# Hybrid retention and attention layer: the mixers' five engines in one written order

## The chip, the cores and the metric

The kernel runs on 1 core of one Trainium2 chip. The metric is the device time of one execution in microseconds (us). The kernel before takes 1167.28 us, the median of 3 runs (1166.82 to 1169.25).

## What is computed

One post-norm encoder layer in f32, with S = 1024 rows, D = 1024 and a hidden width of 2816:

```
u   = x @ W_in                                # one projection: rq rk rv rg aq ak av
ret = swish(rg) * GroupNorm(retention_fwd(rq, rk, rv) + retention_bwd(rq, rk, rv))   # 8 heads of 64
att = windowed attention(aq, ak, av)          # 8 query heads, 2 key/value heads, +-128, ALiBi, sink
h   = LN1(alpha * x + concat(ret, att) @ W_out)
f   = (silu(h @ W_gate) * (h @ W_up)) @ W_down + sigmoid(h @ W_pg) * (p @ W_pe)
out = LN2(alpha * h + f)
```

Retention is computed in chunks: within a chunk by masked scores, between chunks by a state of 64 x 64 that decays (by a scan over the chunks, once forward and once backward).

## The kernel before

**Number format.** A large matmul in f32 is made of three matmuls in a rounded format: each operand is split into a high part (a copy on ACT, which rounds) and a low part (a subtraction on DVE). `mm3` (L82 to L84) is such a triple; three matmuls with 512 columns are here called one projection *step*.

**Stages.** First comes a stretch of projection that is not touched (up to about 50 us). Then come the mixers (to about 350 us): four pairs of heads, each with retention and attention. They are laid between projection steps: `queue` holds all steps of the projections that are left, and `run` goes over a list in which F (None) stands for a *share* of steps, and everything else is a piece of a mixer (the keys' transposes K, the chunk products kv C, the scans S, scores, values, and so on). Pair 0's attention has 16 + 64 steps, pair 0's retention ("retention 0") 48, pairs 1 to 3 have 48 each, and 16 come last. Behind the mixers lie W_out, LN1, the gate, the FFN and LN2.

**Ticks.** `ticks` counts the steps that have been emitted. `take` emits a step and then all pieces in the lists `later` and `side` whose tick has come. `side` carries the splitting of later weights: of W_out (`presplit_out`), of W_pg (`presplit_gate`) and of two small ones (`presplit_small`). Each is loaded, summed where a sum is needed (DVE, L715 for W_pg), split by `put` (high part on ACT L653, low part on DVE L654) and stored to HBM by SP (L655, to `wod` or `pgd`).

**What sets the order.** In the mixers, `manual_schedule` names PE alone (L791): PE runs in the order of the source. What DVE, ACT, POOL and SP do is placed by a scheduler, with an edge (`behind`) from the newest projection step to pieces that shall not come before it. Each engine's queue, in whatever order it ends up, is then run in that order: an instruction that waits holds those behind it. SP issues the DMAs.

**What the steps below name.** L116 loads two tiles of a projection weight (tag "raw", 2 buffers), L76 and L77 split them. L418 and L424 are the keys' transposes and their decayed copies, two half tiles each (K(0), K(1)); L439 is kv, L446 and L448 its evacuation on DVE and ACT, L456 the scan and L467 the DMA that moves states. L577, L579 and L582 are an attention block's scores, their masked reduction and their exponential; L617 and L622 transposes of these and the copies ("ptr"); L634 the values. The norm of retention goes row (L530) to HBM and back: spread (L535), power (POOL, L538), store, fetch (L545), scaled (L549), at the ticks of LAGS = (3, 6, 9, 12, 15) behind it.

## Time and profile before

| | before |
|---|---|
| median of 3 runs | 1167.28 us |
| profiled execution, its time | 1168.96 us |
| its span | 1167.2 us |
| PE busy | 1151.9 us (99%) |
| DVE, ACT, POOL busy | 895.7 (77%), 564.4 (48%), 105.1 (9%) us |
| fp32 triples, first of three lines (L82) | 240 instructions, 97.2 us |

The prediction quotes the views. A row of windows gives the start and end, the length, then busy us and number of instructions for PE, PEld, DVE, ACT and POOL, then the granted clock, the busy share of the DMA engines and GB/s. A row of waits gives the engine and line that waited, what released it, and us in total, times, longest. A row of the timeline gives start, length, engine, line and operation, with the idle time ahead of it in brackets. A row of groups gives count, busy us, mean ns, and idle before. The lines are those of the kernel before.

### The profile page before, as it was taken

Reading aid. Unit: us, or ns where it says so; the run is one execution under the profiler, and the core shown is the slowest. Engines: PE = TensorE matmul, PEld = TensorE weight load, DVE = VectorE, ACT = ScalarE, POOL = GpSimd, SP = SyncE. Lnnn points to the kernel's source line nnn. Section 1 sums busy time; section 2 is a strip of 40 time slices with the busy share of each in tenths; the row PEclk is TensorE's granted clock in tenths of the full one; section 3 lists DMA queues with packets and bytes.
Section 4 is the critical chain, followed back from the end, with each engine's and each line's share of the span. In section 5 each row is a group of like instructions: output and inputs, shape, how many; then the busy total and the mean of one; then the engine's idle time right before and its main releaser. Section 6 shows DMA issues by size and latency. Waiting matters only on the chain.

```text
span 1167.2 us, 19086 instructions
## 1 busy us (share of the span) xinstructions
PE 1151.9 (99%) x6978; PEld 965.8 (83%) x6978; DVE 895.7 (77%) x1687; ACT 564.4 (48%) x1162; POOL 105.1 (9%) x118
## 2 busy tenths in 40 slices
PE   9999999999999999999999999999999999999997
PEld 7888878777888888888888888888888888888886
DVE  5556678594858898948999988888888876774778
ACT  5645367666546366214444433443344445552462
POOL 2000010102010021000000000000000011124242
PEclk9999999999999999999999999999999999999999
DMA  6346777666567955756322332332223289999978
GB/s 251 103 159 214 258 241 232 211 210 194 154 216 241 365 178 185 269 193 210 112 96 98 115 107 98 103 134 101 100 73 136 83 249 344 348 236 217 256 172 233
DMA packets 88863, 218.64 MB, mean 187 GB/s; under 512 B 12544, under 2 KB 20928, under 8 KB 88768
## 3 DMA queue, kind: packets, MB, share of 16 engines
q1 hardware_dynamic: 79984, 200.11, 49.6%
q0 software_dynamic: 8784, 17.31, 8.4%
q8 instruction: 55, 0.90, 0.3%
q14 instruction: 40, 0.33, 0.1%
HBM read 143.35 MB, written 62.19 MB: 176 GB/s over the span
## 4 chain that ended last, share of the span: by engine, by line
PE 89%; issue 4%; DMA 3%; DVE 2%; ACT 1%; SPq 1%; POOL 0%; DVEq 0%; POOLq 0%; ACTq 0%
PE bmm L875 8%; PE bmm L874 8%; PE bmm L876 8%; PE bt L874 6%; PE bt L875 6%; PE bt L876 6%; PE bmm L82 4%; PE bmm L84 4%; PE bmm L83 4%; PE bs L876 4%; PE bs L875 4%; PE bs L874 4%; PE bo L876 4%; PE bo L875 4%; PE bo L874 4%
## 5 line engine op out<-in xcount | busy, mean ns | idle before, releaser
L82 PE MATMUL bmm<-H,w 128*128 128x512 f32 x240 | 97.2, 405 | 0.1
L84 PE MATMUL bmm<-H,w 128*128 128x512 f32 x240 | 94.0, 392 | 0.5 <-issue 0.5
L83 PE MATMUL bmm<-H,w 128*128 128x512 f32 x240 | 94.0, 392 | 0.0
L1474 ACT ACTIVATE ev<-ev 128x512 f32<-128x512 f32 x42 | 26.5, 630 | 105.0 <-DVE ev L1503 91.8
L1648 POOL DMA_DIRECT2D h0b<-in_w_dn x24 | 21.6, 900 | 537.7 <-DVE ev L1454 503.6
L82 PEld LDWEIGHTS bmm<-H,w 128*128 128x128 f32 x240 | 45.2, 188 | 12.2 <-issue 1.9
L84 PEld LDWEIGHTS bmm<-H,w 128*128 128x128 f32 x240 | 45.0, 188 | 10.2
L83 PEld LDWEIGHTS bmm<-H,w 128*128 128x128 f32 x240 | 45.1, 188 | 7.8
L582 ACT ACTIVATE sc<-sc,st 128x384 f32<-128x384 f32 (+1 forms) x64 | 37.3, 586 | 17.1 <-DVE st L579 17.0
L579 DVE CUSTOM_DVE_ANT_0 sc<-cst,bs,nskb 128x384 f32<-128x384 f32 (+1 forms) x64 | 35.2, 575 | 7.0 <-PE bs L578 6.9
L1503 DVE TENSOR_TENSOR ev<-ev,bt 128x512 f32<-128x512 f32 x44 | 30.0, 682 | 12.5 <-PE bt L876 12.5
L622 ACT ACTIVATE ptr<-bt 128x384 f32<-128x384 f32 (+1 forms) x64 | 26.5, 456 | 25.5 <-PE bt L617 25.4
L1454 DVE TENSOR_TENSOR ev<-ev,bs 128x256 f32<-128x256 f32 x63 | 25.5, 416 | 15.6 <-PE bs L876 14.7
L1476 DVE TENSOR_TENSOR ev<-ev 128x512 f32<-128x512 f32 x42 | 29.0, 691 | 10.5 <-ACT ev L1474 9.0
L77 DVE TENSOR_TENSOR w<-raw,w 128x512 fp32r<-128x512 f32 x34 | 23.0, 687 | 17.3 <-ACT w L76 16.7
L874 PE MATMUL bmm<-H,u 128*128 128x512 f32 x92 | 36.1, 392 | 0.0
L875 PE MATMUL bmm<-H,u 128*128 128x512 f32 x92 | 36.0, 392 | 0.0
L876 PE MATMUL bmm<-H,u 128*128 128x512 f32 x92 | 35.8, 389 | 0.0
L874 PE MATMUL bmm<-H,w 128*128 128x512 f32 x84 | 32.9, 392 | 0.0
L875 PE MATMUL bmm<-H,w 128*128 128x512 f32 x84 | 32.9, 392 | 0.0
L876 PE MATMUL bmm<-H,w 128*128 128x512 f32 x84 | 32.7, 389 | 0.0
L1454 DVE TENSOR_TENSOR ev<-ev,bo 128x256 f32<-128x256 f32 x70 | 28.3, 416 | 5.2 <-PE bo L876 4.5
(832 smaller groups left out, 3836.8 us busy)
## 6 DMA issues: line engine op xcount, KB each, us to landing
ad<-ev SPq DMA_DIRECT2D x33, 512.0 KB, 2.6
pgd<-pro SPq DMA_DIRECT2D x28, 512.0 KB, 3.3
raw<-in_w_gu SPq DMA_DIRECT2D x22, 512.0 KB, 4.0
ln<-in_w_gu SPq DMA_DIRECT2D x22, 512.0 KB, 4.6
raw<-ad SPq DMA_DIRECT2D x40, 256.0 KB, 6.2
ln<-ad SPq DMA_DIRECT2D x37, 256.0 KB, 6.3
H<-in_w_dn SPq DMA_DIRECT2D x33, 256.0 KB, 9.2
wod<-aq SPq DMA_DIRECT2D x16, 512.0 KB, 2.7
```

The costliest lines, as they stand in the source:

```text
L82: pe.matmul(o, lh, rh, start=start, stop=False)
L83: pe.matmul(o, lh, rl, start=False, stop=False)
L84: recent[0] = pe.matmul(o, ll, rh, start=False, stop=stop).ins.name
L579: dve.tensor_tensor_reduce(sc[g][:, :nk], cst[:, tc0:tc0 + nk], b[:, :nk], slope(i, g), nskb[:, 2 * i + g:2 * i + g + 1], ALU.add, ALU.min ...
L582: act.activation(sc[g][:, :nk], sc[g][:, :nk], AF.Exp, bias=st_[:, 0, j, g:g + 1], scale=-1.0, accum_out=st_[:, 2, j, g:g + 1])
L622: act.activation(p_[:, :hi - lo, :], tb[:, :hi - lo, :], AF.Copy)
L874: pe.matmul(o, lh, rh, start=start, stop=False, skip_group_check=True)
L875: pe.matmul(o, lh, rl, start=False, stop=False, skip_group_check=True)
L876: pe.matmul(o, ll, rh, start=False, stop=stop, skip_group_check=True)
L1454: dve.tensor_tensor(out_, x, b, ALU.add)
L1476: dve.tensor_tensor(c[:, 1, :], c[:, 0, :], c[:, 1, :], ALU.mult)
L1503: dve.tensor_tensor(get(name), ev[left][:, m, :], right, ALU.add)
```

## The change

From pair 0's attention to the end of the mixers, `manual_schedule` now names all five engines: each one's queue is in the order in which the code emits it, and `behind` with its edges is gone. So that a piece that needs a result comes later in the code, `at(dt, f)` puts f into `later`, dt ticks on, and `due` runs all that has come, in order of tick:

- A projection weight's split (before: emitted with its load) is emitted at ticks 5 (ACT, first half), 6 (DVE), 7 and 8 behind its load; a weight of rv at 2.5 and 3.5.
- `put`: ACT's copy at once, DVE's part one tick later, the store 2.6 ticks later. Where a sum is needed, it is emitted a tick ahead.
- Exponentials come 1 tick behind their scores, the states' move 2 behind the scan, the two swaps of query halves 1.4, the square's low part 1 and 2.5, the gate's product 0.6.
- The second W_out load's puts are at 48.5 and then every 3.6 ticks (before 44 and 4); W_pg's splits every 3.1 ticks (2.8 and 1.9 before), the last seven every 2.7.
- "sn" has 2 buffers (before 1).
- The lists of `run` change: in retention 0, one share (before two) stands between the second key half and kv, and shares go from S_(1, 1), Q and scores; in pairs 1 to 3 the two parts of each direction's scan are back to back, and a share stands behind each direction.

```diff
-    recent = [None]
...
-    def behind(ins):
-
-        tc.add_manual_dep(ins.ins, recent[0], mybir.DependencyInfo(
-            mybir.DependencyClass.NoSync, mybir.DependencyReason.DATA), reason="order")
-        return ins
...
+    def at(dt, f):
+        later.append((ticks[0] + dt, f))
+
+    def due(upto):
+        while True:
+            x = min((x for what in (later, side) for x in what if x[0] <= upto), key=lambda x: x[0], default=None)
+            if x is None:
+                return
+            (later if x in later else side).remove(x)
+            x[1]()
+
     def take(k):
         for _ in range(min(k, len(queue))):
             queue.pop(0)()
             ticks[0] += 1
-            for what in (later, side):
-                for x in [x for x in what if x[0] <= ticks[0]]:
-                    what.remove(x)
-                    x[1]()
+            due(ticks[0])
...
         def load():
-            hold["w"] = unit2(w_mt[idx])
+            r = rawt(2 * HF)
+            sp.dma_start(r, w_mt[idx])
...
+            for i in range(2):
+                for k, f in enumerate((upper, lower)):
+                    if live[0]:
+                        at(5 + 2 * i + k, lambda f=f, i=i: f(i))
...
-                for h in range(2):
-                    sp.dma_start(self.states[rows64(d), h, 1 - d:NCH - d, :], U[rows64(h), 0:NCH - 1, :])
+
+                def move():
+                    for h in range(2):
+                        sp.dma_start(self.states[rows64(d), h, 1 - d:NCH - d, :], U[rows64(h), 0:NCH - 1, :])
+
+                at(2, move)
...
-            sm, r, home = bt([P, 2, 8], "sn", 1), bt([P, HF], ("rb", "kv1")[t]), rnd[2 * self.i + t]
+            sm, r, home = bt([P, 2, 8], "sn", 2), bt([P, HF], ("rb", "kv1")[t]), rnd[2 * self.i + t]
...
     def put(x, o, dst):
-        behind(act.activation(o[:, 0, :], x, AF.Copy))
-        behind(dve.tensor_tensor(o[:, 1, :], x, o[:, 0, :].bitcast(F32), ALU.subtract))
-        sp.dma_start(dst, o.bitcast(F32))
+        act.activation(o[:, 0, :], x, AF.Copy)
+        at(1, lambda: dve.tensor_tensor(o[:, 1, :], x, o[:, 0, :].bitcast(F32), ALU.subtract))
+        at(2.6, lambda: sp.dma_start(dst, o.bitcast(F32)))
...
-        at = [2 + 2.8 * k for k in range(14)] + [60 + 1.9 * k for k in range(7)] + [73 + 1.9 * k for k in range(9)]
+        when = [2 + 3.1 * k for k in range(14)] + [49.5 + 3.1 * k for k in range(7)] + [71.6] + [73.5 + 2.7 * k for k in range(7)]
...
-    with tc.manual_schedule(engines={mybir.EngineType.PE}):
-        enqueue([mtile(0, ev_av), proj_rv(), *project(1), *project(2), *project(3), gate(0), gate(1), gate(2), gate(3)])
-
+    enqueue([mtile(0, ev_av), proj_rv(), *project(1), *project(2), *project(3), gate(0), gate(1), gate(2), gate(3)])
+    live[0] = True
+    ET = mybir.EngineType
+    with tc.manual_schedule(engines={ET.PE, ET.DVE, ET.Activation, ET.Pool, ET.SP}):
...
-        side.extend(presplit_out(1, ops, 44, 4, spare[:1]))
+        side.extend(presplit_out(1, ops, 48.5, 3.6, spare[:1]))
...
-        run([K(0), F, K(1), F, F, C(0), C(1), F, S_(0, 0), S_(0, 1), F, S_(1, 0), S_(1, 1), F, F, F, Q(0), F, (r.scores,), Q(1), F, F,
-             (r.out,), E(0), E(1), F, (decay_q, 1), F, M(0), (decay_k, 1, 0), F, (decay_k, 1, 1), M(1)], 48)
+        run([K(0), F, K(1), F, C(0), C(1), F, S_(0, 0), S_(0, 1), F, S_(1, 0), S_(1, 1), F, Q(0), F, (r.scores,), F, Q(1), F, F,
+             (r.out,), E(0), E(1), F, (decay_q, 1), F, M(0), (decay_k, 1, 0), F, (decay_k, 1, 1), F, M(1), F], 48)
...
-            run([K(0), F, K(1), sco(0), F, *V, C(0), C(1), F, sco(1), S_(0, 0), F, trn(0), sco(2), S_(0, 1), F, trn(1),
-                 sco(3), S_(1, 0), F, val(0), val(1), S_(1, 1), F, trn(2), sco(4), F, trn(3), sco(5), Q(0), F, val(2), val(3),
+            run([K(0), F, K(1), sco(0), F, *V, C(0), C(1), F, sco(1), S_(0, 0), S_(0, 1), F, trn(0), sco(2), S_(1, 0), S_(1, 1), F,
+                 trn(1), sco(3), F, val(0), val(1), Q(0), F, trn(2), sco(4), F, trn(3), (r.scores,), F, sco(5), Q(1), F,
```

Two places show what this moves. In the rows, a line is followed by the operation, what it writes and reads (with the program's buffer numbers), and the shape; x2 is two alike. The first is SP's queue at the start of retention 0: `wod` are stores of W_out's splits, `pre` loads of W_pg, `pgd` the stores of its splits. Before:

```order
L655 DMA wod<-aq_468 128x1024
L655 DMA wod<-pro_469 128x1024
L705 DMA pre_1135<-in_w_pg 128x1024
L705 DMA pre_1136<-in_w_pg 128x1024
L655 DMA wod<-aq_468 128x1024
L705 DMA pre_1137<-in_w_pg 128x1024
L705 DMA pre_1138<-in_w_pg 128x1024
L116 DMA raw_1471<-in_w_mt 128x1024
L655 DMA pgd<-pro_1139 128x1024
```

The change (L694 is L655 of before, L744 is L705, L315 is L116):

```order
L694 DMA wod<-aq_468 128x1024
L694 DMA wod<-pro_469 128x1024
L694 DMA wod<-aq_468 128x1024
L744 DMA pre_1135<-in_w_pg 128x1024
L744 DMA pre_1136<-in_w_pg 128x1024
L744 DMA pre_1137<-in_w_pg 128x1024
L744 DMA pre_1138<-in_w_pg 128x1024
L315 DMA raw_1159<-in_w_mt 128x1024
L694 DMA pgd<-pro_1139 128x1024
```

The first two loads of W_pg now stand behind the last store of W_out.

The second place is DVE's queue in pair 1, from kv's evacuation (COPY) on: SCALAR_TENSOR_TENSOR on `qq` is the forward scan, on `y` the norm's scaling, ISA the score reductions. Before:

```order
L446 COPY qq_1751<-bt_1720 128x7x64
L446 COPY pt_1786<-bs_1755 128x8x64
L456 SCALAR_TENSOR_TENSOR qq_1751<-qq_1751,cd 128x7x64
L579 ISA sc_1803,st_1694<-cst,bs_1805,nskb 128x384
...
L456 SCALAR_TENSOR_TENSOR qq_1751<-qq_1751,cd 128x64 x5
...
L549 SCALAR_TENSOR_TENSOR y_1134<-y_1134,gn,rb_1621 128x8x64
```

The change (L582 is L549 of before, L475 is L446, L323 a projection weight's split, L693 is L654, L612 is L579, L485 is L456, L754 is L715):

```order
L582 SCALAR_TENSOR_TENSOR y_1134<-y_1134,gn,rb_1579 128x8x64
L475 COPY qq_1756<-bt_1725 128x7x64
L475 COPY pt_1791<-bs_1760 128x8x64
...
L485 SCALAR_TENSOR_TENSOR qq_1756<-qq_1756,cd 128x64 x6
...
L485 SCALAR_TENSOR_TENSOR pt_1791<-pt_1791,cd 128x64 x6
L485 SCALAR_TENSOR_TENSOR pt_1791<-pt_1791,cd 128x7x64
L754 TENSOR_TENSOR pre_1136<-pre_1135,pre_1136 128x512
```

The first norm's scaling now stands ahead of kv's evacuation, each scan is in one piece, and the sum for W_pg's next split stands behind both.

## Prediction

> **What bounds the kernel now.** I read the page's busy times, then the windows of the mixers (about 50 to 350 us), then what PE waits for.

> ```profile
> PE 1151.9 (99%) x6978; PEld 965.8 (83%) x6978; DVE 895.7 (77%) x1687; ACT 564.4 (48%) x1162; POOL 105.1 (9%) x118
> ```

> ```profile
> 140.00:160.00 20.00, 19.92 (x260) 16.00 (x259) 15.44 (x27) 10.01 (x19) 0.00 (x0) 1.00 0.91 295
> 160.00:180.00 20.00, 18.14 (x203) 15.14 (x202) 14.19 (x33) 15.33 (x40) 5.62 (x6) 1.00 0.44 149
> 180.00:200.00 20.00, 19.25 (x186) 15.47 (x185) 19.66 (x47) 12.90 (x33) 0.00 (x0) 1.00 0.79 262
> 220.00:240.00 20.00, 17.45 (x212) 14.11 (x211) 13.10 (x27) 13.44 (x35) 2.29 (x2) 1.00 0.60 201
> 280.00:300.00 20.00, 18.90 (x220) 15.53 (x219) 15.04 (x34) 13.27 (x34) 1.63 (x1) 1.00 0.62 201
> 500.00:520.00 20.00, 20.00 (x90) 16.53 (x90) 7.71 (x13) 2.53 (x4) 0.00 (x0) 1.00 0.61 208
> ```

> The columns are window, length, and then busy PE, PEld, DVE and ACT. PE sets the time. In the mixers it stands still for 0.08 + 1.86 + 0.75 + 2.55 + 1.10 = 6.34 us in all; the other windows there are full. So 6.3 us is the most that a new order can win, while a delay of PE has no such limit. The window 500 to 520 shows PE full behind the mixers, where nothing is edited: what PE loses in the mixers stays in the time. The clock is 1.00 in every window.

> ```profile
> PE bt L439 <- ACT pt L424: 1.9, 2, 1.1
> PE bs L577 <- DVE pt L446: 1.7, 1, 1.7
> PE bo L147 <- POOL sq L144: 1.3, 1, 1.3
> ```

> The largest waits are short, and of different kinds: PE is fed almost without a gap by the order that the scheduler found.

> **The change, part by part.** It computes nothing new. It fixes the order on DVE, ACT, POOL and SP as the code emits it; what stands at a queue's head and waits now holds all behind it. So I follow queues: which transfer is at a head, and when PE needs what lies behind. One projection step is three matmuls; rows of the chain give the pace:

> ```profile
> 123.79 0.23 PE bmm L82
> 124.02 0.23 PE bmm L83
> 124.25 0.23 PE bmm L84
> ...
> 128.58 1.02 PE bt L439 x58
> ```

> A step is 0.68 us, and so is a tick of the new table. A share is 2.53 steps in a pair (1.73 us), 3.43 in retention 0 (2.33).

> *Second W_out load, pair 0's attention.* A raw tile is free when its split is done. The split of the projection weight loaded at tick 17 now ends at tick 25, and only then can the second w_out load go. The put that reads it is due on ACT at tick 27: two steps, 1.36 us later, and up to 1.4 more with a turn and a score of the attention between them (a turn's first four transposes stand below, 0.60).

> ```profile
> L684 SPq DMA_DIRECT2D raw<-in_w_out x5: 328/338/509, 59.3 to 289.2; - x5
> DMA to landing us min/median/max: 4.6/5.1/5.5
> L77 DVE TENSOR_TENSOR w<-raw,w 128x512 fp32r<-128x512 f32 x26 | 17.6, 686 | 7.0 <-ACT w L76 6.4 <-DMA states<-qq 0.5
> L622 ACT ACTIVATE ptr<-bt 128x384 f32<-128x384 f32 x48 | 21.2, 483 | 21.4 <-PE bt L617 21.3
> 175.78 0.60 PE L617 MATMUL bt<-cst,sc 128*128 128x128 f32 x4
> ```

> Split 0.69 + issue 0.33 + landing 5.1 = 6.1 against 1.4 to 2.8: ACT stands 3.3 to 4.7 us, and behind it the copies of attention weights (L622) that PE's transposes wait for. Two banks hide about a turn of it. I take **+2.5** (0.5 to 3.6).

> *Start of retention 0.* The first W_pg loads (L705) were issued between stores of W_out; now all four stand behind the last store, which is due at about tick 80, when PE is near 120.5.

> ```profile
> 117.04 2.11 SPq L705 DMA_DIRECT2D pre<-in_w_pg  x2
> L705 SPq DMA_DIRECT2D pre<-in_w_pg x8: 328/450/1395, 114.6 to 200.4; - x8
> DMA to landing us min/median/max: 5.5/6.0/7.8
> 122.03 0.84 ACT L424 ACTIVATE pt<-bt,kd 128x256 f32<-128x256 f32 x2
> 122.74 0.65 ACT L653 ACTIVATE pro<-pre 128x512 fp32r<-128x512 f32 x1
> 123.83 0.84 ACT L424 ACTIVATE qq<-bt,kd 128x256 f32<-128x256 f32 x2 [0.43 <-PE bt L418]
> 124.55 0.84 ACT L424 ACTIVATE pt<-bt,kd 128x256 f32<-128x256 f32 x2
> ```

> The load lands at 120.5 + 6.0 = 126.5. ACT's put (L653) still stands between the copies of the two key halves, so these end at 126.5 + 0.6 + 1.5 = 128.6. PE's kv stood at 128.58, seven steps after the second key half; now three steps are between: 123.79 + 3 × 0.68 = 125.9. **+2.8** (1.2 by the shortest landing and an earlier store, 3.6).

> *Retention 0, kv to out.* Now 24 steps, 16.3 us, and 1.1 of scores and 1.0 of out: 18.4 (before 27.4 steps). DVE has 26 long operations in it and 12 short adds.

> ```profile
> 179.74 0.68 DVE L456 SCALAR_TENSOR_TENSOR qq<-qq,cd 128x448 f32<-128x448 f32 x1
> 180.34 0.68 DVE L654 TENSOR_TENSOR pro<-pre,pro 128x512 fp32r<-128x512 f32 x1
> ...
> 182.61 0.28 DVE L456 SCALAR_TENSOR_TENSOR pt<-pt,cd 128x64 f32<-128x64 f32 x1
> 182.81 0.68 DVE L654 TENSOR_TENSOR pro<-pre,pro 128x512 fp32r<-128x512 f32 x1
> ...
> 175.31 1.57 DVE L456 SCALAR_TENSOR_TENSOR qq<-qq,cd 128x64 f32<-128x64 f32 x5
> ```

> Long operations start 0.60 apart, an add with another's work behind it takes 0.20, and dependent adds back to back 1.57 / 5 = 0.31. That is 26 × 0.60 + 12 × 0.32 = 19.4, and 0.8 for a hand-over from ACT: 20.2 against 18.4. **+2.0** with what kv's delay adds (0 to 3).

> *The norm's way through HBM, pairs 1 to 3.* Fetch at tick 12, scaling at 15: three ticks, 2.0 us, and 0.5 of attention between.

> ```profile
> L545 SPq DMA_DIRECT2D rb<-rnd x8: 459/596/945, 175.4 to 346.0; - x8
> DMA to landing us min/median/max: 2.7/4.0/6.1
>   DVE y L549: 6.7, 5
> 179.07 0.75 DVE L549 SCALAR_TENSOR_TENSOR y<-y,gn,rb 128x512 f32<-128x512 f32 x1 [0.94 <-DMA rb<-rnd]
> ```

> Issue 0.6 + landing 4.0 = 4.6 against 2.5: DVE's head stands 2.1 us (0 by the shortest, 4.2 by the longest). Before it waited here too, 6.7 us in five, but the scaling stood late: in pair 1 behind most of the first scan. Now it is ahead of kv's evacuation and of the score reductions, whose banks PE waits for. I count **+2.1** once in each pair (PE meets the rest later, when DVE has caught up). [...]

> *Pair 1's scans and gate split.* ACT's put of a sum waits for the sum on DVE, which now stands behind both scans.

> ```profile
> L715 DVE TENSOR_TENSOR pre<-pre,pre 128x512 f32<-128x512 f32 x12 | 8.5, 704 | 0.1
> L653 ACT ACTIVATE pro<-pre 128x512 fp32r<-128x512 f32 x28 | 17.6, 630 | 17.1 <-DMA pgd<-pro 13.5 <-DVE pre L715 2.8 <-DVE qq L456 0.6
> L579 DVE CUSTOM_DVE_ANT_0 sc<-cst,bs,nskb 128x384 f32<-128x384 f32 x47 | 27.3, 608 | 6.7 <-PE bs L578 6.7
> ```

> DVE from kv's evacuation to that sum: 1.2 evacuation, 4 × 0.6 splits, 2 × 1.2 reductions, two scans of 2 × 0.60 + 6 × 0.32 = 3.1, and the sum 0.6, in all 12.8; ACT's put and copy 1.3 more, 14.1. PE reaches the values that need the copy after four shares (6.9), three scores (2.2) and 2.7 of kv, turns and values: 11.8. **+2.3**. ACT's key copies, late before kv (1.9 above), stay late, and the put between them adds 1.6. Pair 1 with its norm: 2.1 + 2.3 + 1.6 = **+6.0** (1 to 9.7). In pairs 2 and 3 the un-mixed scans cost 12 × (0.31 − 0.20) = 1.3 more, of which I take 1.1: **+3.2** each with the norm (0 to 6). [...]

> *What is won.*

> ```profile
> SPq L655 <- DVE pro L654: 45.3, 24, 5.5
> SPq L655 <- DVE aq L654: 34.5, 14, 6.5
> ```

> Stores are placed 1.6 ticks behind their split and hold SP less than these 80 us; the second "sn" buffer frees the second norm. The even gate split takes load off the stretch 180 to 200, where DVE has 19.66 of 20. POOL has 9% of work and no new one. I grant all of PE's stalls but pair 1's at kv: 6.34 − 1.9 = **−4.4**. The matmuls of kv, scores and out are the same before and after, and moving the half copies and the exponentials by a tick lies under PE's steps as long as ACT, at 13 to 15 of 20 us, is not held by a load: 0.

> Sum: 2.5 + 2.8 + 2.0 + 6.0 + 3.2 + 3.2 − 4.4 = **+15.3** on the profiled execution's 1168.96, that is 1184.3. That execution lay 1.7 above the median of the runs, so the median should be about **1182.5 us**.

> **Rivals.** *The lag compounds.* DVE never makes good what it loses, and every upper bound is met: 3.6 + 3.6 + 3.0 + 9.7 + 6 + 6 − 4.4 = +27.5, 1194.8. For it: DVE is at 14 to 19 of 20 us in the pairs. Against: in 140 to 160 and 220 to 240 it has 5 to 7 us free.

> *Only the loads bite.* DVE's free quarter hides the norms and scans of all pairs; the two loads, retention 0 and pair 1's copies stay: 2.5 + 2.8 + 2.0 + 3.9 − 4.4 = +6.8, 1174.

> *The other side: the even feed wins.* The place is DVE's stretch 180 to 200 with SP's queue behind it. If stores no longer at SP's head let loads land as early as the shortest rows (4.6, 5.5, 2.7 us), the waits are 0.5 + 1.2 + 1.0 and the stalls of before go: 2.7 − 6.3 = −3.6, 1163.7; with none of the waits, 1161. It decides from the point where a norm's fetch lands in 2.5 us and a W_pg load in under 4. Against: no L705 row is under 5.5.

> *It hardly changes the order.* The scheduler may already have stood near the source's order, with gains and waits that cancel: 1165 to 1169.6. Against: the rows of SP, ACT and DVE differ at every place followed above.

> **How the numbers follow.** Sum as worked out (about 1175 to 1191) 0.48; compounding 0.17; only the loads 0.17; even feed 0.12; no change 0.06. The likeliest gives 1182.5, with its own range 1175 to 1191. Leaving out most of the even feed (0.10) and the upper half of compounding (0.08) gives 1166 to 1202. A difference under 0.2% (2.3 us) can't be told from none: faster 0.12, same 0.06, slower 0.82.

> **What would show it.** PE's waits after: a wait of kv (bt) for ACT's key copies of 2 to 3 us near 125; transposes (bt) waiting for ACT's ptr copies near 77, with ACT idle on the raw<-in_w_out load; score banks (bs) waiting for DVE in each pair, with DVE idle on rb<-rnd or kv<-rnd; in pair 1 values (bo) waiting for ptr. PE's idle in the mixers would be about 21 us. Loads that have landed when ACT reaches them, PE's idle under 6 us, or DVE idle on no norm would prove the steps wrong one by one; a stretch behind the mixers that is longer than before would break the premise that only the mixers count.

## The result, and the profile after

The changed kernel takes 1199.78 us (median of 6 runs, 1197.57 to 1200.41); the kernel before, on the same chip, 1167.51. The ratio is 1.0271 (95% interval 1.0258 to 1.0285): 32 us slower. Slower was forecast, but by 15 us, and the time lies inside the range of 1166 to 1202 only at its upper end. Three of the executions behind this text (one each of the kernel before, of "PE alone" and of the filler below) took 1.6 to 2 times as long as the others of their kernel and are in no median and no ratio.

The profiled execution has a span of 1198.0 us, 30.8 more than before. The first row is the page's of the kernel after, then come its windows (columns as before):

```profile
PE 1164.3 (97%) x6978; PEld 974.1 (81%) x6978; DVE 899.9 (75%) x1687; ACT 565.7 (47%) x1162; POOL 105.1 (9%) x118
```

```profile
140.00:160.00 20.00, 12.49 (x161) 10.08 (x160) 14.57 (x27) 5.39 (x9) 0.00 (x0) 0.84 0.62 190
160.00:180.00 20.00, 20.00 (x151) 16.47 (x148) 12.47 (x19) 11.84 (x25) 2.73 (x5) 0.91 0.73 252
180.00:200.00 20.00, 14.73 (x172) 11.78 (x171) 13.46 (x34) 11.89 (x31) 2.58 (x2) 0.91 0.55 163
200.00:220.00 20.00, 18.33 (x169) 14.43 (x169) 16.46 (x38) 11.15 (x29) 0.00 (x0) 0.91 0.60 196
300.00:320.00 20.00, 16.15 (x199) 12.95 (x198) 9.19 (x17) 13.26 (x33) 5.19 (x6) 0.91 0.65 220
320.00:340.00 20.00, 17.41 (x95) 14.07 (x94) 17.69 (x45) 9.41 (x27) 0.00 (x0) 0.91 0.43 136
```

Two things are to be seen. PE stands idle: over the first 400 us its busy time is 392.28 before (first row) and 373.85 after (second row), so 18.4 us more idle.

```profile
0.00:400.00 400.00, 392.28 (x3228) 321.78 (x3229) 277.81 (x562) 227.12 (x520) 30.94 (x37) 1.00 0.64 215
```

```profile
0.00:400.00 400.00, 373.85 (x3092) 304.62 (x3093) 255.54 (x521) 215.77 (x500) 30.84 (x37) 0.97 0.57 191
```

And the granted clock, 1.00 in every window before, is 0.84 to 0.91 in the six windows shown. In 160 to 180 PE is full and gets through 151 instructions. The same 6978 matmuls keep PE busy for 1164.3 us in place of 1151.9: 12.4 more. 18.4 + 12.4 is the whole difference of 30.8.

What PE waits for, in the kernel after (L656 is L617 of before, L661 L622, L610 L577, L612 L579, L468 L439, L453 L424, L475 L446; L525 and L537 make the second queries and use them in out):

```profile
PE bo L537 <- DVE rb L525: 7.2, 1, 7.2
PE bt L656 <- ACT ptr L661: 5.0, 2, 3.8
PE bs L610 <- DVE st L612: 4.6, 3, 2.6
PE bt L468 <- ACT pt L453: 3.6, 3, 1.6
PE bo L673 <- ACT ptr L661: 1.7, 1, 1.7
PE bs L610 <- DVE pt L475: 1.3, 1, 1.3
```

And the waits of ACT and DVE behind them, for transfers (L692 is a put, L320 a projection weight's split, L582 the norm's scaling):

```profile
ACT w L320 <- DMA raw<-in_w_mt: 17.0, 7, 5.3
ACT pro L692 <- DMA pgd<-pro: 10.5, 6, 4.7
ACT pro L692 <- DMA raw<-in_w_out: 4.3, 1, 4.3
```

```profile
DVE w L323 <- ACT w L320: 12.8, 3, 5.2
DVE y L582 <- DMA rb<-rnd: 12.0, 3, 5.6
```

Before, the waits for projection weights (ACT) and for the norm's fetch (DVE) were these:

```profile
ACT w L76 <- DMA raw<-in_w_mt: 5.0, 3, 1.9
```

```profile
DVE y L549 <- DMA rb<-rnd: 4.6, 3, 2.7
```

From PE's timelines: the stages start at the first transposes of keys; the last projection step of the mixers closes pair 3's row (355.5 us before, 386.2 after); what follows it takes 811.7 and 811.8 us. The column "of this idle" is the part of the difference in which PE stands idle.

| stage | before | after | longer | of this idle | forecast |
|---|---|---|---|---|---|
| up to retention 0 | 120.7 | 122.8 | 2.1 | 1.2 | 2.5 |
| retention 0 | 41.8 | 53.6 | 11.8 | 8.4 | 4.8 |
| pair 1 | 61.6 | 68.6 | 7.0 | 3.5 | 6.0 |
| pair 2 | 60.6 | 66.2 | 5.6 | 3.1 | 3.2 |
| pair 3 to the last mixer step | 70.9 | 75.1 | 4.2 | 2.1 | 3.2 |
| stalls of before that go | | | | | −4.4 |

### The profile page after: what moved, and what is told of

It is laid out like the page before. It is cut to its first block, busy times and chain, and to the rows that moved or that the text cites. A ratio compares the mean times of both kernels' runs of the same rounds, so it can differ in the third digit from the quotient of the medians.

```text
span 1198.0 us, 19067 instructions
## 1 busy us (share of the span) xinstructions
PE 1164.3 (97%) x6978; PEld 974.1 (81%) x6978; DVE 899.9 (75%) x1687; ACT 565.7 (47%) x1162; POOL 105.1 (9%) x118
## 4 chain that ended last, share of the span: by engine, by line
PE 78%; DVE 3%; DMA 2%; ACT 1%; issue 1%; SPq 0%; DVEq 0%; ACTq 0%
PE bmm L921 8%; PE bmm L922 8%; PE bmm L923 8%; PE bt L921 6%; PE bt L922 6%; PE bt L923 6%; PE bs L923 4%; PE bs L922 4%; PE bs L921 4%; PE bo L923 4%; PE bo L922 4%; PE bo L921 4%; PE bmm L80 2%; PE bmm L82 2%; PE bmm L81 2%
## 5 line engine op out<-in xcount | busy, mean ns | idle before, releaser
L80 PE MATMUL bmm<-H,w 128*128 128x512 f32 x240 | 99.7, 416 | 0.0
L82 PE MATMUL bmm<-H,w 128*128 128x512 f32 x240 | 95.6, 399 | 0.5 <-issue 0.5
L81 PE MATMUL bmm<-H,w 128*128 128x512 f32 x240 | 95.8, 399 | 0.0
L1521 ACT ACTIVATE ev<-ev 128x512 f32<-128x512 f32 x42 | 26.5, 632 | 105.1 <-DVE ev L1550 91.9
L80 PEld LDWEIGHTS bmm<-H,w 128*128 128x128 f32 x240 | 46.2, 193 | 12.5 <-issue 2.6
L82 PEld LDWEIGHTS bmm<-H,w 128*128 128x128 f32 x240 | 46.1, 192 | 10.7
L81 PEld LDWEIGHTS bmm<-H,w 128*128 128x128 f32 x240 | 46.5, 194 | 8.0
L612 DVE CUSTOM_DVE_ANT_0 sc<-cst,bs,nskb 128x384 f32<-128x384 f32 (+1 forms) x64 | 34.5, 578 | 5.0 <-PE bs L611 4.9
L1523 DVE TENSOR_TENSOR ev<-ev 128x512 f32<-128x512 f32 x42 | 29.1, 692 | 10.5 <-ACT ev L1521 9.0
L661 ACT ACTIVATE ptr<-bt 128x384 f32<-128x384 f32 (+1 forms) x64 | 26.4, 458 | 15.8 <-PE bt L656 15.7
L693 DVE TENSOR_TENSOR pro<-pre,pro 128x512 fp32r<-128x512 f32 x28 | 19.5, 697 | 19.0 <-ACT pro L692 18.5
L692 ACT ACTIVATE pro<-pre 128x512 fp32r<-128x512 f32 x28 | 17.7, 632 | 33.5 <-issue 14.9
L921 PE MATMUL bmm<-H,w 128*128 128x512 f32 x84 | 32.9, 392 | 0.0
L922 PE MATMUL bmm<-H,w 128*128 128x512 f32 x84 | 32.9, 392 | 0.0
L923 PE MATMUL bmm<-H,w 128*128 128x512 f32 x84 | 32.7, 389 | 0.0
```

The costliest lines, as they stand in the source:

```text
L80: pe.matmul(o, lh, rh, start=start, stop=False)
L81: pe.matmul(o, lh, rl, start=False, stop=False)
L82: pe.matmul(o, ll, rh, start=False, stop=stop)
L612: dve.tensor_tensor_reduce(sc[g][:, :nk], cst[:, tc0:tc0 + nk], b[:, :nk], slope(i, g), nskb[:, 2 * i + g:2 * i + g + 1], ALU.add, ALU.min ...
L661: act.activation(p_[:, :hi - lo, :], tb[:, :hi - lo, :], AF.Copy)
L921: pe.matmul(o, lh, rh, start=start, stop=False, skip_group_check=True)
```

## The clock: fixed windows

In finer windows the clock of the kernel after changes at 153.6, 163.8, 184.3, 187.7, 204.8, 208.2, 307.2, 310.6, 331.1 and 334.5 us. All these lie whole multiples of 3.41 us apart. So I cut the trace into windows of that grid:

```profile
150.19:153.60 3.41, 0.32 (x11) 0.18 (x6) 2.03 (x4) 1.01 (x2) 0.00 (x0) 0.99 0.78 298
153.60:157.01 3.41, 0.00 (x0) 0.00 (x0) 2.86 (x5) 1.88 (x4) 0.00 (x0) 0.50 0.28 115
157.01:160.42 3.41, 2.54 (x37) 2.24 (x40) 1.89 (x4) 0.75 (x2) 0.00 (x0) 0.50 0.78 254
160.42:163.84 3.42, 3.42 (x68) 3.01 (x69) 0.92 (x2) 1.50 (x3) 0.00 (x0) 0.51 1.03 279
163.84:167.25 3.41, 3.41 (x16) 2.78 (x16) 2.80 (x5) 3.38 (x7) 0.00 (x0) 1.00 0.92 317
...
187.73:191.14 3.41, 2.11 (x9) 1.27 (x9) 1.96 (x4) 1.93 (x4) 0.00 (x0) 1.00 0.51 181
191.14:194.55 3.41, 3.41 (x18) 2.98 (x19) 3.34 (x9) 2.09 (x6) 0.00 (x0) 1.00 0.42 155
...
201.39:204.80 3.41, 1.74 (x20) 1.19 (x20) 3.40 (x8) 2.03 (x6) 0.00 (x0) 0.99 0.47 112
204.80:208.21 3.41, 3.41 (x12) 2.40 (x10) 2.98 (x7) 2.13 (x6) 0.00 (x0) 0.51 0.83 265
```

The window from 150.19 is 91% idle, and the next one runs at half clock. The one from 187.73 is 38% idle, and the next runs at full clock; the one from 201.39 is 49% idle, and the next at half. The same cut through 13 kernels of this study gives 39 windows at full clock that are followed by half clock; every one was 49% idle or more (the ends of PE's spans are modelled, so such a share is an estimate). Of the windows that were 59% idle or more all were followed by half clock, of those of 48% or less none, between them both occur. The way back differs: the windows at half clock that were followed by full clock were 11% idle or less; all with 14% or more, and one with 10%, were followed by another at half clock. In the kernel after, six windows at half clock hold 2.54 + 5 × 3.41 us of PE's work. A matmul with 512 columns starts 0.43 us behind the one before it in the window from 204.8, and 0.23 once the clock is back at 1.00. So about half of that work is loss, by my estimate 9.8 us of the 12.4. The other 2.6 I can't place; PE's spans are modelled at their ends, and the run with SP alone in order, below, has 2.2 us more of PE's busy time than the kernel before without any half clock.

## The experiments

The theory when they began: the written order puts pieces that wait for transfers at the heads of ACT and DVE; the waits cost PE 18 us, and the clock the rest. The rivals: PE's new lists cost by themselves; DVE simply has too much work; the fall of the clock has another cause than idle time. Ratios are to the kernel before, run beside each; it took 1166.3 to 1168.6 us there. So a difference from the 1199.78 us of the change is given in medians, and where it matters by the ratios too (0.001 is 1.2 us).

**PE alone in source order, all else of the change kept.**

```diff
-    with tc.manual_schedule(engines={ET.PE, ET.DVE, ET.Activation, ET.Pool, ET.SP}):
+    with tc.manual_schedule(engines={ET.PE}):
```

> The changed kernel, but only PE is held to the source's order in the mixers; DVE, ACT, POOL and SP are placed by the scheduler as before. All else of the change stays: the lists of pieces, the ticks at which pieces are emitted, the sn buffers. Theory 'the written order of the four other engines is the cause': PE's idle falls from 26 us to near 8 as before, no long fall of the clock, 1167 to 1173. Rival 'PE's own new order (three steps instead of seven ahead of kv, shorter way to out) is the cause': above 1185.

1.0100 (1.0055 to 1.0146), from runs of 1174 to 1185 us, between what the two theories gave: about half to four fifths of the loss is gone, but not all. Its DVE shows one reason. Without the edges the scheduler puts the scaling ahead of kv's evacuation:

```profile
173.72 0.75 DVE L582 SCALAR_TENSOR_TENSOR y<-y,gn,rb 128x512 f32<-128x512 f32 x1 [4.41 <-DMA rb<-rnd]
```

**The same with `behind` put back.**

```diff
+        recent[0] = pe.matmul(o, ll, rh, start=False, stop=stop).ins.name
...
+                behind(dve.scalar_tensor_tensor(y, y, gn[:, self.i:self.i + 1], r.rearrange("p (n c) -> p n c", c=CH),
+                                                ALU.mult, ALU.mult))
```

> The kernel with only PE held to the source's order, with the edges of before added again (a piece may not be placed ahead of the newest projection step); the new lists and ticks stay. Without the edges the scheduler had put the norm's scaling ahead of kv's evacuation, where DVE waited 4.41 us and PE 10.1 us in three. Theory 'a wait for a load at a queue's head is the cause, whoever puts it there': these waits go, PE's idle falls under 10 us, no half clock, 1165 to 1171. Rival 'the new lists cost by themselves': stays above 1176.

1.0007 (0.9994 to 1.0020), no half clock in the profiled run. So the new lists, ticks, gate spacing and the second sn buffer cost and win nothing that can be told; all 32 us come from fixing the order of the four other engines in place of the scheduler with its edges. This is the base of the next three, which add one engine each.

**SP, DVE or ACT in source order on this base.** The edit for DVE; those for SP and ACT name that engine in its place.

```diff
-    with tc.manual_schedule(engines={ET.PE}):
+    with tc.manual_schedule(engines={ET.PE, ET.DVE}):
```

> The kernel at 1.0007 of before (only PE in source order, edges kept, new lists and ticks) with SP also in source order. Theory 'heads that wait for loads on ACT and DVE': SP's order alone moves loads and stores by a few us but lets ACT and DVE go around them: 1169 to 1174. Rival 'SP's order (stores ahead of loads) is the root of the late loads': 1180 or more.

> The same base with DVE in source order beside PE, ACT, POOL and SP left to the scheduler. Theory 'heads on DVE': the scaling ahead of kv's evacuation and the un-mixed scans are back, DVE waits over 8 us for norms and PE over 10 us in all, with one or two half-clock windows: 1180 to 1188. Rival: DVE's order costs little by itself, 1167 to 1173.

> The base at 1.0007 of before (only PE in source order, edges kept, new lists and ticks) with ACT in source order beside PE. SP's order alone cost 0.75%, DVE's 1.70%. Theory 'heads that wait for loads': ACT's puts and weight splits wait for W_out's, W_pg's and the projection weights' loads, over 15 us in all, and PE waits for key copies and ptr copies behind them: 1176 to 1184. Rival 'DVE's order is the whole cause': 1167 to 1171.

SP 1.0075 (1.0047 to 1.0103), DVE 1.0170 (1.0148 to 1.0192), ACT 1.0062 (1.0047 to 1.0077): 9, 20 and 7 us. Together that is 36, near the 32 of all at once; whether the three simply add up is not shown, and POOL was not tried alone. SP's 1176.56 us lie between what the two theories gave; its trace, of one of the two shorter executions (1174.26; two took 1179), shows no half clock and no wait of PE over 1.3 us, so what the longer ones lose stays open. DVE's 1188.20 is the largest, at the upper edge of what was expected, and ACT's 1174.42 is just below its range. What PE and DVE wait for with DVE alone in order:

```profile
PE bo L545 <- DVE rb L533: 4.9, 1, 4.9
PE bs L618 <- DVE pt L483: 4.4, 3, 3.4
PE bs L618 <- DVE st L620: 4.2, 2, 2.8
```

```profile
DVE pro L701 <- ACT pro L700: 21.9, 16, 3.7
DVE y L590 <- DMA rb<-rnd: 13.6, 3, 7.2
```

Its head waits for the norm as expected, and longer still for ACT's half of the splits (21.9 us; 12.2 on the base): the low part now has a fixed place behind a copy that itself waits, for sums (6.8 us), for stores of earlier splits (6.7) and for other things.

**The norm's scaling later.**

```diff
-LAGS = (3, 6, 9, 12, 15)
+LAGS = (3, 6, 9, 12, 19)
```

> The changed kernel with one number altered: the norm's scaling is emitted at tick 19 behind the norm, not 15 (LAGS 3, 6, 9, 12, 19). Theory 'loads at queue heads': DVE's 14.6 us of waits for the norm's fetch go nearly to nothing, the score banks' waits for DVE (4.6 + 1.3 us of PE's idle) fall to under 2, and with them one or two of the five falls of the clock, 1.8 us each: 5 to 8 us faster, about 1193. Rival 'DVE has too much work there, the wait is slack': time within 2 us of 1199.8.

1197.26 us, 1.0261 (1.0239 to 1.0283): 2.5 us faster than the change by the medians, 1.2 by the ratios, whose intervals overlap. DVE's wait for the norm (12.0 us; the rest of the 14.6 was the attention's) is gone from its list, but the scores still wait for DVE, 3.9 us in two. So no gain can be told, and the rival fits as well as the theory.

**The projection weights' splits later.**

```diff
-                        at(5 + 2 * i + k, lambda f=f, i=i: f(i))
+                        at((5 + 2 * i + k) if ticks[0] < 20 else 9 + 2 * i + k, lambda f=f, i=i: f(i))
```

> The changed kernel with the projection weights' splits (all but the first weight's) emitted at ticks 9 to 12 behind their load, not 5 to 8. 5 ticks are 3.4 us, and the loads took 4.3 / 6.9 / 7.0 us to land. Theory 'loads at queue heads': ACT's 17.0 us of waits for these loads fall under 5, the 7.25 us wait in retention 0 and the 3.77 us wait in pair 3 fall by half or more, and their clock falls go: 7 to 12 us faster, 1188 to 1193. Rival 'the raw buffer is then held too long': the two-buffered raw tiles come free 2.7 us later, the W_out and W_pe loads behind them start later, and the waits only change their name: within 3 us of 1199.8.

1200.40 us, 1.0289: no gain. ACT's wait for these weights is gone from the top of its list, and in its place stand these:

```profile
ACT pro L692 <- DMA pgd<-pro: 13.9, 6, 4.6
ACT aq L692 <- issue: 12.0, 4, 6.8
ACT pro L692 <- DVE pre L754: 7.8, 4, 4.1
```

PE's wait ahead of retention 0's out is 5.9 us, not 7.2, and a new one of 3.5 stands in front of a norm. The rival was right here.

**W_pg's second pair of loads later.**

```diff
-        load(1)
...
+        return [(ticks[0] + 9.5, lambda: load(1))] + [(ticks[0] + t, f) for t, f in zip(when, k0 + k1 + k2 + k3, strict=True)]
```

> The changed kernel with W_pg's second pair of loads issued 9.5 ticks later, so that at retention 0's start two loads of 512 KB (not four) stand ahead of the projection weight's. That weight landed 8.0 us after its issue, with the DMA engines full from 124 to 132 us; ACT waited 3.81 us for it and DVE 5.21. Theory 'bytes ahead of the weight': it lands about 3 us earlier, kv's evacuation and the scans start 3 us earlier, the wait ahead of out falls from 7.25 to about 4 us and one half-clock window goes: 5 us faster, 1195. Rival 'the later loads hold it up anyway (the stores that ACT waits for, the next weight)': within 2 us of 1199.8.

1196.41 us, 1.0239 (1.0224 to 1.0255): 3.4 faster, and the wait ahead of out 4.9. ACT starts on the weight 6.3 us after its issue, not 8.0. The bytes ahead of the weight account for 2.3 us of that wait.

**These three at once.**

> The changed kernel with three edits at once: the norm's scaling at tick 19, the projection weights' splits at ticks 9 to 12, W_pg's second pair of loads 9.5 ticks later. Alone they gave -2.5, +0.6 and -3.4 us. Theory 'each wait hides the next': together more than the sum, -8 to -12 us, 1188 to 1192. Rival 'other waits bound the way (ACT's puts for their stores, the un-mixed scans on DVE)': the sum or less, 1194 to 1199.

1198.22 us, 1.0278 (1.0255 to 1.0302): not even the gain of the last one alone. Its PE waits 3.6 us ahead of a norm, as with the later splits, and 5.4 ahead of out: what is moved at one head comes up at another.

**W_pg's splits further apart.**

```diff
-        when = [2 + 3.1 * k for k in range(14)] + [49.5 + 3.1 * k for k in range(7)] + [71.6] + [73.5 + 2.7 * k for k in range(7)]
+        when = [2 + 3.6 * k for k in range(14)] + [52 + 2.9 * k for k in range(7)] + [71.6] + [73.5 + 2.7 * k for k in range(7)]
```

> The changed kernel with W_pg's first 14 splits 3.6 ticks apart (not 3.1), the next seven from tick 52, 2.9 apart. ACT's puts waited 10.5 us for the store of the put before last, one of them 4.65 us just ahead of retention 0's out, with DVE standing behind it. Theory 'the chain of put, split, store and landing holds the heads': the wait ahead of out falls from 7.25 to 4 to 5 us, and one half-clock window with it: 4 to 6 us faster, about 1195. Rival 'the load of the projection weight holds them': within 2 us of 1199.8.

1202.32 us, 1.0305 (1.0290 to 1.0320), 2.5 slower, with 6.5 us of wait ahead of out: the theory on the chain of puts does not hold as the main cause.

**The two scan directions mixed.**

```diff
+        def scan2(self, part):
+            a, b = [], []
+            self.scan(0, part, a)
+            self.scan(1, part, b)
+            for f, g in zip(a, b):
+                f()
+                g()
...
-                dve.scalar_tensor_tensor(to, frm, by, to, ALU.mult, ALU.add)
+                todo.append(lambda: dve.scalar_tensor_tensor(to, frm, by, to, ALU.mult, ALU.add))
```

> The changed kernel with the adds of the two scan directions taken in turn (first halves of both, a share later the second halves of both). Nothing else moves. Theory 'adds in one piece cost DVE 0.32 us each, mixed ones 0.20': 1.4 us less of DVE's time in each of four stages, and PE's waits for DVE behind the scans fall: 4 to 8 us faster, 1192 to 1196. Rival 'DVE waits at its head anyway, so its work does not count': within 2 us of 1199.8.

1194.86 us, 1.0239 (1.0222 to 1.0256): 4.9 us faster than the change by the medians, inside what was expected, and 3.7 by the ratios, just under it. In each stage the 16 operations of the scans take DVE 4.7 us in place of 6.5. The gain lies almost all in pair 1 (64.8 us in place of 68.6, with one window at half clock less); pairs 2 and 3 gain 0.6 and 0.2. Retention 0 is at 53.1, with 7.0 us of wait ahead of out, so its DVE is held by waits more than by the adds; in pair 1 DVE's work is part of the cause. The edit also ends the forward scan a share later and starts the backward one a share earlier; that was not tested apart.

**A filler in PE's long wait.**

```diff
             self.o = o = [bank("o", (P, NT, CH)) for _ in range(2)]
+            if self.i == 0:
+                for _ in range(24):
+                    pe.matmul(o[0].rearrange("p n c -> p (n c)"), xs[0][:, 0, :P], xs[0][:, 0, :HF], start=True, stop=True)
```

> The changed kernel, with 24 matmuls of 512 columns added on PE just ahead of retention 0's out; nothing reads what they write. PE waits there 7.25 us for the second queries, and 24 x 0.23 = 5.5 us of added work lies inside that wait. Theory 'idle PE loses its clock': in the changed kernel the granted clock stands at 0.50 from 153.2 to 163.4, and 5.65 us of PE's work in it run at half speed. With the filler the clock stays at 1.00 there, and the time falls by 2.8 us, to about 1197. Rival 'the low clock has another cause than idle time (the kind of work, chance)': the clock still falls there and the time stays at 1199.8 or rises a little.

> The kernel with the 24 added matmuls once more, for its profile. The granted clock of three kernels changes only at multiples of 3.41 us, and falls to one half in the window behind one in which PE stood idle for about half of it or more. Theory 'idle PE loses its clock': no half clock between 150 and 165 us here, PE's work after the wait at full rate; then the 3 us that the timed runs are longer must come from more idle time further on, or from the wait itself growing by the added work. Rival: half clock there in spite of a busy PE.

1203.01 and 1202.76 us: 3 slower, where 2.8 faster was expected. The profile of the second:

```profile
140.00:160.00 20.00, 17.61 (x192) 14.25 (x191) 15.15 (x29) 5.38 (x9) 0.00 (x0) 1.00 0.61 181
160.00:180.00 20.00, 18.66 (x146) 15.01 (x146) 11.86 (x18) 11.01 (x23) 2.45 (x5) 1.00 0.71 251
```

The clock is 1.00 where it was 0.84 and 0.91: the fall at this place is caused by PE's idle time. But retention 0 is only 1.6 us shorter, and pairs 2 and 3 are 5.2 us longer, with a window at half clock more; nothing was changed there. That PE comes sooner to places where ACT and DVE are not ready would fit, but is not shown. So the clock's loss is real where it stands, and the time at the end need not fall by it.

**A wait of known size in the kernel before.**

```diff
+            if self.i == 0:
+                z = bt([P, P], "sq", 1)
+                for _ in range(6):
+                    pool.tensor_tensor(z, self.pt[:, 0, 0:2].rearrange("p n c -> p (n c)"), ident, ALU.mult)
+                pe.transpose(o[0].rearrange("p n c -> p (n c)")[:, :P], z, ident)
```

> The kernel before, with a chain of 6 products of 128x128 on POOL (0.43 us each in its profile) that starts from retention 0's scores, and one transpose of its result on PE ahead of out; nothing else reads it. PE should wait there about 1.4 us. Theory 'fixed windows of 3.41 us, half of one idle': 1.4 us is 41% of a window, so no half clock; the loss is the wait alone, +1.0 to +1.6 us. Rival 'every wait of PE also costs clock': +3 us or more.

> The same with 15 products: PE should wait about 5.8 us. Theory 'fixed windows, half of one idle': one or two windows of 3.41 us at half clock behind it, 1.7 us each where PE works through them; the loss is 5.8 + 1.7 to 3.4 = 7.5 to 9.2 us if nothing behind it takes the delay up. Rival 'the clock does not matter to the end, since the other engines gain what PE loses': +5.8 us or less, with the half clock seen.

```profile
PE bo L505 <- POOL sq L504: 2.2, 1, 2.2
```

```profile
PE bo L505 <- POOL sq L504: 8.0, 1, 8.0
```

The first row is of the short chain, the second of the long one; both waits are longer than planned (1.4 and 5.8). With 2.2 us no half clock is seen in the profiled run, which took 1169.83; the ten runs spread from 1168.14 to 1176.97 (ratio 1.0035, 1.0018 to 1.0052), about 4 us in the mean, nearer to the rival's 3 or more than to the theory's 1.0 to 1.6. That a wait of 2.2 us fills most of one window in some runs and is shared by two windows in others would explain the spread, but it is not shown: the longest run has a mean clock of 0.997, and the kernel before has 0.996 to 0.999 without the wait. With 8.0 us the clock is at half from 156.2 to 163.0, and pair 1 starts 10.4 us later than before: 8.0 and, by the same estimate, about 1.9 for the two windows. At the end of the mixers it is 5.6 later; pairs 1, 2 and 3 are 2.9, 1.3 and 0.6 shorter, with that much less idle time of PE in them. The ratio is 1.0072 (1.0050 to 1.0094), 8 us; the profiled execution is the shortest of four.

**A version that might beat both.** The base with edges, and the scaling at tick 20.

> The base at 1.0007 of before with the norm's scaling at tick 20, not 15: a version that could beat both. In the base PE waits 1.4 us for a reduction and 1.2 us for reciprocals on DVE in the pairs. Theory 'less on DVE's way to the scores': PE's idle falls by 1 to 2 us, 1165 to 1167. Rival: those waits come from the work on DVE, not from the scaling: 1167 to 1170, no difference to tell.

0.9998 (0.9990 to 1.0007): no difference. None of the kernels tried is faster than the one before.

## Why the prediction was wrong

The side was right, and so were the place (all in the mixers, and what follows them unchanged at 811.7 and 811.8 us) and the kind of cause (a transfer awaited at a queue's head; of the three repairs of such waits only that of W_pg's loads gained clearly). The sum of PE's idle, forecast at +15.3, was +18.4. Of this, retention 0 has 8.4 (4.8 forecast); the other stages together have 9.9 against 10.5, but, with the stalls that go taken off where they lay, each of them misses by 0.6 to 2.2 us, so that they meet in the sum is in part luck. The size failed on two steps, of which the first is larger.

- **"What PE loses in the mixers stays in the time"** was taken to be all that a wait costs. The text read the clock as 1.00 and left it there. Five stretches of waits, two of them with only 1.7 us of idle time in their window, put PE at half clock for six windows of work: 9.8 us, by the estimate above, that no term had. This is what the profiled run has lost; by the filler, winning it back at one place need not shorten the time. The rows of before do not show it: their longest stall is 1.7 us, and the clock stays at 1.00.
- **"Retention 0, kv to out: +2.0"** was 7.2. The term counted DVE's work and, but for 0.8 us, took its operands as there. The rows of the kernel after show what was left out:

```profile
122.61 2.26 SPq L744 DMA_DIRECT2D pre<-in_w_pg  x4
124.93 0.44 SPq L315 DMA_DIRECT2D raw<-in_w_mt  x1
```

```profile
132.92 0.64 ACT L320 ACTIVATE w<-raw 128x512 fp32r<-128x512 f32 x1 [3.81 <-DMA raw<-in_w_mt]
133.46 0.62 ACT L692 ACTIVATE pro<-pre 128x512 fp32r<-128x512 f32 x1
133.98 0.58 ACT L477 ACTIVATE qq<-bt 128x512 f32<-128x512 f32 x1
```

```profile
133.59 0.69 DVE L323 TENSOR_TENSOR w<-raw,w 128x512 fp32r<-128x512 f32 x1 [5.21 <-ACT w L320]
134.20 0.62 DVE L475 COPY qq<-bt 128x448 f32<-128x448 f32 x1
```

```profile
130.03 1.10 PE L468 MATMUL bs<-rv,pt 64*64 64x64 f32 x60
157.75 0.47 PE L537 MATMUL bo<-rb,states 128*64 128x64 f32 x2 [7.25 <-DVE rb L525]
```

```profile
150.91 0.63 ACT L692 ACTIVATE pro<-pre 128x512 fp32r<-128x512 f32 x1 [4.65 <-DMA pgd<-pro]
```

```profile
151.57 0.69 DVE L693 TENSOR_TENSOR pro<-pre,pro 128x512 fp32r<-128x512 f32 x1 [2.78 <-ACT pro L692]
```

  The next projection weight is issued behind the four W_pg loads that the text did place there, and ACT can start on it only 8.0 us after its issue; its split stands ahead of kv's evacuation on both engines. Five ticks are 3.4 us, and the rows of these loads before gave 4.1 to landing at the least:

```profile
L116 SPq DMA_DIRECT2D raw<-in_w_mt x14: 332/337/748, 20.2 to 309.2; - x14
DMA to landing us min/median/max: 4.1/4.8/6.6
```

  The prediction followed this split for the buffer that it frees, and not for what it holds up. The rows also say where the 7.2 us lie. PE ends kv at 131.1, and DVE comes to its evacuation at 134.2, 3.1 late and directly behind the split that waited 5.21: here a waiting head did hold what stood behind it. From there to PE's use of the second queries at 157.7 are 23.5 us, of which DVE stands 4.1 behind ACT's puts (0.75, 2.78 and 0.55); the other 19.4 are its work, as the term had it. PE takes 19.4 from kv's end to its wait. So the work was right, and 3.1 for the load and 4.1 for the puts were not counted. What each would win is less clear: the load order is worth 2.3 us, but wider puts left 6.5 of the 7.2, since waits came up elsewhere. With DVE alone in order the same wait is 4.9, while later splits and mixed adds left 5.9 and 7.0.

The other terms, one by one. **Second W_out load**: ACT stood 4.3 us (3.3 to 4.7 forecast), the stage is 2.1 longer (2.5). **Start of retention 0**: the load did hold the key copies, but the put waited only 2.05 us and PE's kv 0.95 (2.8 forecast). PE itself came 2.1 late from the stage before, so the two terms cover each other in part and should not have been added. **The norm**: DVE waited 12.0 us in three, more than the 6.3 counted; the longest, in pair 1, is

```profile
189.18 0.75 DVE L582 SCALAR_TENSOR_TENSOR y<-y,gn,rb 128x512 f32<-128x512 f32 x1 [5.64 <-DMA rb<-rnd]
```

  Yet moving it gave no gain that can be told (2.5 us by the medians, 1.2 by the ratios), not 6.3: the wait ahead of out and the scores' waits stay at 6.9 and 3.9. **Pair 1**: 7.0 (6.0 forecast), of which two windows of clock make 3.4 by the same estimate; the idle time is only 3.5 longer, so that 7.0 is so near to 6.0 is luck. **Un-mixed scans**: mixing them saved DVE 1.8 us a stage, more than the 1.3 of the term, and 4.9 us of time (3.7 by the ratios); the term had 1.1 in each of pairs 2 and 3, where 0.6 and 0.2 were won, and a part of pair 1's 2.3, where 3.9 were, so its mechanism is shown and its size is not. **What is won, −4.4**: the stalls of before are indeed replaced, but nothing was won beside them; with PE alone in order, the edges and the same lists and spacing the time is that of before.

The rival "compounding" at 1194.8 was nearest in time, by a wrong mechanism: not DVE's lag but the clock and one late load. "Even feed wins" fell: SP's waits for splits rose (62.1 and 41.7 us for the two put tiles, before 45.3 and 34.5).

## What to carry to other kernels

When an order is fixed by hand on an engine that reads transfers, compare each piece's place (in time behind its issue) with the slowest landing in the trace and not the median alone (here 3.4 us behind the issue, where the projection weights took 4.3 to 7.0 to land), and list what stands behind it; an edge that only keeps a piece from coming too early leaves the scheduler free to go around a late one. Waits at different heads can hide one another (three repairs at once won 1.6 us here by the medians, one of them alone 3.4), so they are neither added up in a forecast nor removed one by one in a repair. A forecast of idle PE needs a second term for its clock, which here went with how the idle time fell into windows of 3.41 us.
